# Loading Q and K of the first pairs on two queues, dummy matmuls in TensorE's idle time, and newly searched orders, in a cosine-similarity attention

## The chip, the core and the metric

The kernel runs on one core of one Trainium2 chip. The metric is the device time of one execution in microseconds (us); lower is better. A profile comes from one execution, and its span is about 1.7 us shorter than the time of that same execution (195.7 against 197.39 us for the kernel before, 192.3 against 194.01 for the changed one), so spans are compared only with spans and times only with times.

Runs over 1.5% above the fastest run of the same kernel count as slow and are left out. Two runs are compared as a ratio with a 95% interval, from fast runs of the same rounds.

## The reference, cut to what matters

```python
batch, heads, seq, dim = 8, 12, 512, 64          # Q, K, V: float32, random; tau = 0.1
Q_norm = Q / (np.linalg.norm(Q, axis=-1, keepdims=True) + 1e-10)
K_norm = K / (np.linalg.norm(K, axis=-1, keepdims=True) + 1e-10)
scores = np.einsum('bhqd,bhkd->bhqk', Q_norm, K_norm) / tau
weights = np.exp(scores - np.max(scores, axis=-1, keepdims=True))
weights = weights / (np.sum(weights, axis=-1, keepdims=True) + 1e-10)
return np.einsum('bhqk,bhkd->bhqd', weights, V).astype(np.float32)
```

There are 96 independent heads with 512 rows of 64 each. Each head needs 512 x 512 exponentials, and these are the bulk of the work of ScalarE, which is busy for 94% of the span (its timeline is below).

## The kernel before: the parts that matter

The kernel takes the heads two at a time, as 48 "pairs". Each pair goes through this chain (the short names are those of the printed orders below):

| name | what | engine |
|---|---|---|
| LD.s.0, LD.s.1, LV.s | load Q, K, V of pair s, 256 KB each | a DMA queue |
| SQ | squares of Q and K | GpSimd, in the first pairs also ScalarE |
| SSQ, RED | sums of the squares: 16 matmuls against an identity, then a reduction | TensorE, VectorE |
| LN, EX | 1/norm by logarithm and exponential, pairs 0 and 1 only (later: Newton steps on VectorE) | ScalarE |
| SCL | Q and K scaled to bf16 | VectorE, GpSimd |
| TR, EVA | transposes, and their eviction | TensorE, VectorE |
| SCO.s.c | block c of 4 of the scores: 2 matmuls | TensorE |
| EXP.s.c | exponentials of that block, a 128x1024 tile | ScalarE |
| PV, RCP, NRM, ST | product with V, division by the sums, store | TensorE, VectorE, a DMA queue |

Pair 0 is special. To start early, its K is not scaled ahead of the transposes; the exponential applies 1/norm instead, as a scale for each partition. The partitions of a score tile are 128 rows of K, and the two heads that stand side by side in a tile of 128x1024 ("full tile") need different scales. So the program gives pair 0 eight tiles of 128x512 ("half tiles", 0.69 us each in the trace below) where the others have four full ones.

Every engine executes a fixed, printed list of operations, found earlier by a search. The program adds semaphore waits only where an operation needs another engine's result. So an operation waits for its own operands, and also for **everything ahead of it in its engine's list** (in the trace below the operands of pair 0's first scores are ready at 8.64 us, and these run at 11.48, behind what is listed ahead of them). That second wait is what most of this study is about.

```python
    P.add("table", "act", [], lambda e: e.preload_act_table_set("natural_log_exp_and_others"))
    P.add("wz", "dve", [], lambda e: e.memset(warm_in[:, :], 0.0))
    for k in range(WARM):                                  # WARM = 32
        P.add(("warm", k), "pe", ["wz", ("warm", k - 1) if k else None],
              lambda e: e.matmul(out=sc_ps[:, 3, 0:256], lhsT=warm_in[:, 0:128], rhs=warm_in[:, :], start=True, stop=True))
    ...
        # head of pair 0: K on SyncE's queue
        P.add(("LD", 0, 1), "sp", [], lambda e: e.dma_start(out=qk[0][:, 1], in_=src(K, 0)), slot="first2")
    ...
            # loads of the other pairs: pair 1 on ScalarE's queue, pairs 1 and 2 held back by dummies
            for w, x in ((0, Q), (1, K)):
                P.add(("LD", s, w), "act" if s == 1 else "sp",
                      [key(n, s - R_QK, *y) for n in ("SCL", "SQ") for y in ((w,), (0,), (w, 0), (w, 1))]
                      + [("warm", 2) if s == 1 else ("warm", 9) if s == 2 else None],
                      lambda e, w=w, x=x: e.dma_start(out=qk[iq][:, w], in_=src(x, s)), slot=...)
    ...
ORDER = {
    "sp":  LD.0.1 LD.0.0.1 LD.0.0.0 LD.3.1 LD.2.0 LD.2.1 LD.4.0 ...
    "act": table LD.1.1 LD.1.0 SQ.0.0.1 SQ.0.0.0 SCL.0.1 LN.0.0 EX.0.0 SQ.3.1 SQ.1.0 LN.0.1 EX.0.1 LN.1 EX.1.1 EX.1.0
           EXP.0.0.0 ... EXP.0.2.0 SQ.3.0 EXP.0.2.1 ...
    "pe":  warm.0 ... warm.21 TR.0.1 TR.0 warm.22 ... warm.26 SSQ.1 warm.27 ... warm.30 SCO.0.0 warm.31 SSQ.2 SCO.0.1 TR.1 ...
```

The "warm" matmuls, called dummies below, compute nothing that is used. They are there to keep TensorE busy while it waits for the first data: in the trace below its granted clock falls to 0.50 at 8.56 us, after 3.41 us in which it was busy for 1.66 us.

## Time and profile before

| | us |
|---|---|
| time, median of 3 runs | 196.32 (195.83 to 197.01) |
| span of the profiled run (its time was 197.39) | 195.7 |
| first half tile of pair 0 starts | 12.13 |
| first of the 187 full tiles starts | 18.17 |
| the 187 full tiles, from their start to that of the last three half tiles | 172.8 |
| from there to the end of the span ("tail") | 4.7 |

The last four rows add up to the span (12.13 + 6.04 for pair 0 + 172.79 + 4.74 = 195.7), since ScalarE's exponentials are the one stream that is nearly unbroken from the first score block to the end. Everything else matters only where it delays this stream. Note that the profiled run was about 1.1 us above the median of the timed runs; that matters for the reading of the result.

These are lines of the page of the kernel before: the span, the granted TensorE clock (the share of full rate that the profile records, in tenths) in 40 equal slices, the group of the full tiles (busy us, mean ns | idle just before them, and its cause), the chain of work that ended last, by engine, and two DMA issues with their us to landing.

```profile
span 195.7 us, 7082 instructions
...
PEclk9859999999999999999999999999999999999999
...
ACT 58%; PE 13%; DMA 11%; POOL 7%; DVE 7%; SPq 2%; issue 2%; DVEq 0%; POOLq 0%
...
L451 ACT ACTIVATE et<-scps 128x1024 bf16<-128x1024 f32 x187 | 171.9, 1125 | 1.2 <-PE scps L429 1.2
...
qk<-in_K_dram ACTq DMA_DIRECT2D x1, 256.0 KB, 5.1
qk<-in_Q_dram ACTq DMA_DIRECT2D x1, 256.0 KB, 6.2
```

The full tiles waited only 1.2 us in 173, so a gain has to come from ahead of 18.17 us. The third clock slice (9.8 to 14.7 us) reads 5: TensorE ran at half its rate there. The two loads of pair 1, issued on ScalarE's queue, took 5.1 and 6.2 us to land.

The timeline of ScalarE before (start us, length us, engine, line, operation, out<-in, shapes, count; in brackets the idle time ahead of it and what ended it):

```profile
1.96 0.42 ACTq L377 DMA_DIRECT2D qk<-in_K_dram  x1
2.41 0.49 ACTq L377 DMA_DIRECT2D qk<-in_Q_dram  x1
...
8.46 1.15 ACT L226 ACTIVATE sq<-qk 128x512 bf16<-128x512 f32 x2 [1.47 <-DMA qk<-in_K_dram]
...
12.13 1.26 ACT L441 ACTIVATE et<-scps,xr 128x512 bf16<-128x512 f32 x2 [0.62 <-PE scps L429]
13.85 1.26 ACT L441 ACTIVATE et<-scps,xr 128x512 bf16<-128x512 f32 x2 [0.46 <-PE scps L429]
15.36 0.69 ACT L441 ACTIVATE et<-scps,xr 128x512 bf16<-128x512 f32 x1 [0.24 <-PE scps L429]
15.95 0.62 ACT L226 ACTIVATE sq<-qk 128x512 bf16<-128x512 f32 x1
16.46 1.83 ACT L441 ACTIVATE et<-scps,xr 128x512 bf16<-128x512 f32 x3
18.17 36.75 ACT L451 ACTIVATE et<-scps 128x1024 bf16<-128x1024 f32 x40
...
190.96 1.32 ACT L447 ACTIVATE et<-scps 128x512 bf16<-128x512 f32 x3
```

Pair 1's loads are issued only at 1.96 and 2.41 us. The two squares at 8.46 are pair 3's K and, behind it, pair 1's Q; they end at 9.6. Pair 0's half tiles stall three times (0.46, 0.24, and 0.62 ahead of the first), and a square of pair 3 (0.62 at 15.95) stands among them.

The timeline of TensorE before, same columns:

```profile
9.66 1.03 PE L243 MATMUL xps<-sq,ident 128*128 128x64 bf16 x16 [0.91 <-ACT sq L226]
10.51 1.04 PE L219 MATMUL scps<-warm_in 128*128 128x256 bf16 x4
11.48 0.61 PE L429 MATMUL scps<-qt 64*128 64x512 bf16 x2
```

Pair 0's first scores start at 11.48. They stand in the list behind pair 1's sums (9.66), which waited for ScalarE's square, and behind four dummies. ScalarE had the norms by then and waited 0.62 us for these scores, so that part of the delay is the four dummies'. So the first exponential of pair **0** is set by the loads and squares of pair **1**, and by dummies that stand in front of needed work. Two lines of a table of stretches show the clock (stretch, length, then busy us and instruction count of TensorE, its weight loads, VectorE, ScalarE and GpSimd; then granted clock, DMA share, GB/s):

```profile
5.37:8.78 3.41, 1.64 (x16) 0.86 (x13) 2.37 (x5) 1.61 (x5) 1.43 (x2) 0.97 1.06 367
8.78:12.20 3.42, 2.54 (x23) 1.52 (x24) 0.88 (x2) 1.70 (x8) 2.71 (x3) 0.50 1.09 346
```

TensorE was busy for 1.64 of 3.41 us, and then ran at a clock of 0.50. (The trace's record of the clock has the fall at 8.56 us, just inside the first stretch, and the return to full rate at 15.38. In the 3.41 us up to the fall, from the record's entry at 5.14 us on, TensorE was busy for 1.66 us.)

### The profile page before, as it was taken

What the parts mean: (1) busy time and instruction counts of PE and PEld (TensorE: products, weight loads), DVE (VectorE), ACT (ScalarE), POOL (GpSimd) and SP (SyncE); (2) the same over time, 40 slices, a digit from 0 to 9 for tenths busy, and PEclk for the clock granted to TensorE, in tenths of its full rate; (3) what the DMA queues carried; (4) which work ended last, traced back from release to release, by engine and by line L of the source; (5) the groups of instructions that cost most, each with busy time, mean ns of one, the idle gap of its engine ahead of it and who ended that gap; (6) DMA issues with size and microseconds to landing.
All of it is one profiled execution on the core that took longest, in us unless ns stands there. A gap on an engine that the chain in (4) does not pass through costs nothing.

```text
span 195.7 us, 7082 instructions
## 1 busy us (share of the span) xinstructions
PE 180.5 (92%) x2932; PEld 117.3 (60%) x2932; DVE 149.9 (77%) x450; ACT 183.2 (94%) x212; POOL 161.2 (82%) x148
## 2 busy tenths in 40 slices
PE   7497999999999999999999999999999998999992
PEld 5264676665666666656666665666665665556552
DVE  1448989987888888777888896888797886878534
ACT  3559999999999999999999999999999998999993
POOL 3499899798879999999997999899899969954200
PEclk9859999999999999999999999999999999999999
DMA  4999999999998999999998899569992680555454
GB/s 124 354 348 348 349 344 307 353 195 279 372 381 297 270 297 359 348 344 261 368 383 264 206 358 315 170 173 321 285 318 65 172 282 10 162 153 145 164 170 157
DMA packets 56240, 51.71 MB, mean 264 GB/s; under 512 B 6928, under 2 KB 56208, under 8 KB 56208
## 3 DMA queue, kind: packets, MB, share of 16 engines
q1 hardware_dynamic: 55520, 50.67, 82.9%
q10 hardware_dynamic: 688, 0.59, 1.0%
q8 instruction: 23, 0.38, 0.9%
q14 instruction: 9, 0.07, 0.1%
HBM read 37.75 MB, written 12.58 MB: 257 GB/s over the span
## 4 chain that ended last, share of the span: by engine, by line
ACT 58%; PE 13%; DMA 11%; POOL 7%; DVE 7%; SPq 2%; issue 2%; DVEq 0%; POOLq 0%
ACT et L451 55%; PE scps L429 4%; DMA out_dram<-ob 4%; DMA qt<-qn 4%; PE ops L467 3%; DMA qk<-in_K_dram 3%; POOL qn L267 3%; PE xps L243 3%; POOL sq L228 3%; DVE ob L481 2%; DVE qt L419 1%; ACT et L441 1%; PE xps L274 1%; POOL vb L456 1%; ACT sq L226 1%
## 5 line engine op out<-in xcount | busy, mean ns | idle before, releaser
L451 ACT ACTIVATE et<-scps 128x1024 bf16<-128x1024 f32 x187 | 171.9, 1125 | 1.2 <-PE scps L429 1.2
L228 POOL TENSOR_TENSOR sq<-qk 128x1024 bf16<-128x1024 f32 (+1 forms) x48 | 86.9, 1822 | 8.1 <-DMA qk<-in_K_dram 5.2
L429 PE MATMUL scps<-qt 64*128 64x512 bf16 x384 | 75.5, 390 | 4.8 <-ACT et L451 3.1
L467 PEld LDWEIGHTS ops<-vb,et 128*128 128x128 bf16 x1504 | 53.4, 98 | 27.5 <-issue 21.7
L467 PE MATMUL ops<-vb,et 128*128 128x65 bf16 x1504 | 68.4, 195 | 0.9 <-DVE nps L250 0.5
L267 POOL TENSOR_TENSOR qn<-qk,rk 128x512 bf16<-128x512 f32 x44 | 45.3, 1043 | 9.6 <-DVE rk L343 9.5
L481 DVE TENSOR_TENSOR ob<-ops,rd 128x512 f32<-128x512 f32 x47 | 32.5, 691 | 2.1 <-DMA out_dram<-ob 0.7
L267 DVE TENSOR_TENSOR qn<-qk,nps 128x512 bf16<-128x512 f32 x48 | 32.1, 681 | 0.4
L419 DVE COPY qt<-xps 128x1024 bf16<-128x1024 bf16 (+1 forms) x47 | 30.3, 645 | 2.2 <-PE xps L274 1.6
L456 POOL TENSOR_SCALAR vb<-vf 128x512 bf16<-128x512 f32 x48 | 29.5, 627 | 2.8 <-DMA vf<-in_V_dram 2.8
L429 PEld LDWEIGHTS scps<-qt 64*128 64x128 bf16 x384 | 18.6, 93 | 21.5 <-ACT et L451 7.7
L274 PE MATMUL xps<-ident,qn 128*128 128x128 bf16 x352 | 28.3, 223 | 0.7 <-DVE qn L267 0.7
L243 PE MATMUL xps<-sq,ident 128*128 128x64 bf16 x624 | 25.8, 195 | 3.1 <-ACT sq L226 1.9
L243 PEld LDWEIGHTS xps<-sq,ident 128*128 128x128 bf16 x624 | 21.4, 98 | 11.1 <-issue 4.2
L274 PEld LDWEIGHTS xps<-ident,qn 128*128 128x128 bf16 x352 | 20.2, 99 | 10.1 <-DVE rd L479 3.6
L479 DVE RECIPROCAL rd<-ops 128x8 f32<-128x8 f32 x47 | 9.7, 207 | 17.9 <-PE ops L467 16.9
L250 DVE TENSOR_REDUCE nps<-xps 128x16 f32<-128x64 f32 x38 | 8.8, 231 | 8.1 <-PE xps L243 7.7
L237 DVE TENSOR_REDUCE nps<-sq 128x8 f32<-128x512 bf16 x16 | 10.9, 684 | 0.0
L338 DVE TENSOR_TENSOR nps<-nps,ys 128x32 f32<-128x32 f32 (+1 forms) x48 | 9.3, 194 | 1.1
L339 DVE SCALAR_TENSOR_TENSOR nps<-nps,ys 128x32 f32<-128x32 f32 (+1 forms) x48 | 9.3, 194 | 1.1
L219 PE MATMUL scps<-warm_in 128*128 128x256 bf16 x32 | 6.7, 383 | 1.1 <-DVE warm_in L216 1.1
L226 ACT ACTIVATE sq<-qk 128x512 bf16<-128x512 f32 (+1 forms) x5 | 2.6, 539 | 4.7 <-DMA qk<-in_Q_dram 3.2
(40 smaller groups left out, 43.3 us busy)
## 6 DMA issues: line engine op xcount, KB each, us to landing
vf<-in_V_dram SPq DMA_DIRECT2D x48, 256.0 KB, 6.3
qk<-in_K_dram SPq DMA_DIRECT2D x47, 256.0 KB, 6.2
out_dram<-ob SPq DMA_DIRECT2D x47, 256.0 KB, 4.7
qk<-in_Q_dram SPq DMA_DIRECT2D x46, 256.0 KB, 6.4
qk<-in_Q_dram SPq DMA_DIRECT2D x2, 128.0 KB, 3.2
qk<-in_K_dram ACTq DMA_DIRECT2D x1, 256.0 KB, 5.1
qk<-in_Q_dram ACTq DMA_DIRECT2D x1, 256.0 KB, 6.2
out_dram<-ob SPq DMA_DIRECT2D x1, 128.0 KB, 1.7
```

The lines of the kernel that those rows point to most:

```text
L228: emit = lambda e: e.tensor_tensor(out=b, in0=a, in1=a, op=ALU.mult)
L237: lambda e, w=w: e.tensor_reduce(out=dst(w), in_=sq[s % R_SQ][:, 8 * w : 8 * w + 8, :], axis=AX.X, op=ALU.add))
L243: last = e.matmul(out=x_ps[:, 0:64], lhsT=ident[:, :], rhs=sq[s % R_SQ][:, :, 4 * k : 4 * k + 4], start=(k == 0), stop=(k == 15))
L267: lambda e: e.tensor_tensor(out=qn[iqn][:, w].rearrange("p t h d -> p h t d"), in0=qk[iq][:, w].rearrange("p h (t d) -> p h t d", t=NT), i ...
L274: last = e.transpose(dst[:, i, :], qn[s % R_QN][:, b // NT, b % NT].rearrange("p h d -> p (h d)"), ident[:, :])
L419: lambda e: e.tensor_copy(out=qt[iqt][:, :].rearrange("p w t x -> p (w t) x")[:, 0:nb], in_=tb[:, 0:nb]))
L429: last = e.matmul(out=sc_ps[:, 2 * b + h, :], lhsT=qt[iqt][64 * h : 64 * h + 64, 1, c, :], rhs=qt[iqt][64 * h : 64 * h + 64, 0, :, :], sta ...
L451: lambda e, c=c, b=b: e.activation(out=et[iet][:, c, :, :], in_=sc_ps[:, 2 * b : 2 * b + 2, :], func=ACT.Exp, scale=inv_tau))
L456: lambda e: e.tensor_scalar(out=vb[:, iq, :, :, 0:DIM].rearrange("p c h d -> p h c d"), in0=vf[iv][:, :, :].rearrange("p h (c d) -> p h c ...
L467: last = e.matmul(out=o_ps[:, h, 65 * t : 65 * t + 65], lhsT=et[iet][:, c, h, 128 * t : 128 * t + 128], rhs=vb[:, iq, c, h, :], start=(c = ...
L479: lambda e: e.reciprocal(out=rd[io][:, :], in_=grid[:, :, :, DIM]))
L481: lambda e: e.tensor_tensor(out=ob[io][:, :], in0=grid[:, :, :, 0:DIM], in1=rd[io][:, :].unsqueeze(3).to_broadcast([128, 2, NT, DIM]), op= ...
```

## The change

The intent is threefold: to load Q and K of pairs 0 to 2 at once and in the order of need, K on ScalarE's queue and Q on SyncE's, with no dummy holding a load back; to keep TensorE's clock up by placing the dummies in its predicted idle time up to the first product with V; and to search the printed orders anew, with that load order kept. The core of the diff, with cuts marked by dots:

```
-    for k in range(WARM):
-        P.add(("warm", k), "pe", ["wz", ("warm", k - 1) if k else None],
-              lambda e: e.matmul(out=sc_ps[:, 3, 0:256], lhsT=warm_in[:, 0:128], rhs=warm_in[:, :], start=True, stop=True))
+    def dummy(key, bank, needs):
+        P.add(key, "pe", needs, lambda e: e.matmul(
+            out=bank[:, 0:256], lhsT=warm_in[:, 0:128], rhs=warm_in[:, :], start=True, stop=True))
+    for k in range(WARM):
+        dummy(("warm", k), sc_ps[:, 3], ["wz", ("warm", k - 1) if k else None])
...
-        P.add(("LD", 0, 1), "sp", [], lambda e: e.dma_start(out=qk[0][:, 1], in_=src(K, 0)), slot="first2")
+        P.add(("LD", 0, 1), "act", [], lambda e: e.dma_start(out=qk[0][:, 1], in_=src(K, 0)), slot="first2")
...
-                P.add(("LD", s, w), "act" if s == 1 else "sp",
-                      [key(n, s - R_QK, *y) for n in ("SCL", "SQ") for y in ((w,), (0,), (w, 0), (w, 1))]
-                      + [("warm", 2) if s == 1 else ("warm", 9) if s == 2 else None],
+                P.add(("LD", s, w), "act" if w and s < 3 else "sp",
+                      [key(n, s - R_QK, *y) for n in ("SCL", "SQ") for y in ((w,), (0,), (w, 0), (w, 1))],
...
+    for k in range(sum(FILL)):
+        dummy(("fill", k), *((sc_ps[:, 3], ["wz"]) if k < FILL[0] else (o_ps[:, 0], [("EVA", 0, 1)])))
...
-SQ_ON = {1: ('act', 'pool'), 2: ('act', 'pool'), 3: ('act', 'pool')}
+SQ_ON = {1: ('act', 'pool'), 2: ('act', 'pool')}
-WARM = 32
+WARM = 19
+FILL = (9, 16)
...
 "sp":
-  LD.0.1 LD.0.0.1 LD.0.0.0 LD.3.1 LD.2.0 LD.2.1 LD.4.0 ...
+  LD.0.0.0 LD.0.0.1 LD.1.0 LD.2.0 LV.0 LD.3.1 LD.3.0 ...
 "act":
-  table LD.1.1 LD.1.0 SQ.0.0.1 SQ.0.0.0 SCL.0.1 LN.0.0 EX.0.0 SQ.3.1 SQ.1.0 LN.0.1 EX.0.1 LN.1 EX.1.1 EX.1.0 EXP.0.0.0 ...
+  table LD.0.1 LD.1.1 LD.2.1 SQ.0.0.1 SQ.0.1 LN.0.0 EX.0.0 LN.0.1 SQ.1.1 EX.0.1 SQ.2.1 LN.1 EX.1.0 EX.1.1 EXP.0.0.0 ...
 "pe":
-  warm.0 .. warm.21 TR.0.1 TR.0 warm.22 .. 26 SSQ.1 warm.27 .. 30 SCO.0.0 warm.31 SSQ.2 SCO.0.1 TR.1 SCO.0.2 ...
+  warm.0 .. warm.18 fill.0 TR.0.1 fill.1 .. 4 TR.0 fill.5 .. 8 SSQ.1 SCO.0.0 SCO.0.1 SSQ.2 fill.9 .. 15 TR.1 SCO.0.2
+  fill.16 17 SCO.0.3 fill.18 .. 23 SCO.1.0 SSQ.3 fill.24 PV.0.0.0 ...
 "sp", its end:
-  ST.44 ST.39 ST.45 ST.43 ST.46 ST.47.0 ST.47.1
+  ST.44 ST.39 ST.45 ST.46 ST.42 ST.47.1 ST.47.0
```

Cut here: the waits of a few operations on certain dummies, which now name the last warm-up dummy or are gone; six squares and scales of pairs 0 to 2 that swap ScalarE and GpSimd; and the rest of the printed lists, which the search reordered throughout. Pair 3's squares go to GpSimd as one operation.

> **What bounds the kernel.** ScalarE's exponentials. ScalarE's timeline shows the first half tile at 12.13 us, the eight halves of pair 0 until 18.17, then 187 full tiles until 190.96 (172.8 us, 0.924 each; 0.918 in the chain's longest unbroken stretch, 61.53 us for 67), then 4.7 us of tail. ScalarE's waits put only 1.2 us in front of the full tiles: what can be won lies before 18.17.
>
> **The head before.** Pair 1 decides it. Its loads are held back by dummy matmuls, issued on ScalarE's queue at 1.96 and 2.41 us, and take 5.1 and 6.2 us (DMA issues). DMA moves only 111 to 297 GB/s from 3.5 to 5.5 us (windows). ScalarE's squares (pair 3's K ahead of pair 1's Q) end at 9.6, pair 1's sum matmuls run 9.66 to 10.69, and pair 0's scores stand behind them and four dummies in TensorE's order: 11.48, although their operands were ready at 8.64. The granted clock is 0.5 from about 8.8 to 14 us: 16 sum matmuls take 1.03 us instead of 0.64, eight transposes 1.03 instead of 0.62.
>
> **What changes.** K of pairs 0 to 2 goes on ScalarE's queue, Q on SyncE's, without holds, ahead of other loads. [...] I count on earlier issue and order, not bandwidth. K of pair 0 follows the table load; before's trace has a ScalarE issue at 1.96, ahead of that load's end at 2.06, so I expect it near 1 us. Pair 3's two squares leave ScalarE (0.52 in the stream of pair 0) for GpSimd (1.9 us). 25 fill matmuls follow 19 warm-up ones; they cost time only where TensorE is on the chain: seven stand between pair 2's sums and pair 1's transposes, 0.8 us at full clock, 1.5 at half. [...]
>
> **On the critical path (estimates from those durations).** Pair 1 landed about 7.1; its sums end about 8.5; pair 2's square on ScalarE (landed about 8.5) stands before pair 1's logarithm; first exponential about 9.8 (-2.3). Pair 0 in 5.2 us instead of 6.0 (square gone, a short stall left): first full tile about 15.0 (-3.2). The full tiles lose about 0.5: GpSimd (3.55 us per pair against ScalarE's 3.68) and VectorE have less lead, so pairs 3 to 6 may stall. Tail unchanged.
>
> **Predicted: 193.5 us**, range 191.8 to 195.5. Faster by over 2%: 0.25; within 2%: 0.72; slower by over 2%: 0.03.
>
> **Right or wrong in the profile.** First exponential between 9 and 10.5 us; first full tile 14.3 to 16; K of pair 0 issued near 1 us; granted clock 1.0 from 9 to 14 us, with 0.6 us sums and transposes; 187 full tiles in 172.5 to 174 us; ScalarE's idle in front of them 1 to 2.5 us.
>
> **What would make it wrong.** Landing times: nine loads outstanding within 4 us may delay pairs 1 and 2. K of pair 0 may wait for the table load (+1 us). TensorE may still be throttled. The new order may lack slack in pairs 2 to 6 and give the gain back as stalls. If landings are quick and nothing stalls: 191.5, over 2%.

Two passages are cut from the prediction because no trace or run of this case showed what they rest on. No term of its sum is among them: -2.3, -0.8 and +0.5 us stand, about -2.7 unrounded, which leads from the 196.32 us of before to about 193.5. That the second queue brings no bandwidth was the author's assumption at that point; experiment 3 tests it. The 0.8 and 1.5 us for seven dummies are estimates of the author's: in before's trace the first 22 dummies took 4.53 us, 0.206 each and so 1.4 for seven. In the trace of the changed kernel, at a granted clock of 1.00, the seven took 0.93 us (at 10.10).

## The result, and the profile after

| | before | after |
|---|---|---|
| time, median (range) | 196.21 us (195.83 to 197.01), 4 runs | 193.87 us (193.34 to 194.07), 4 runs |
| span of the profiled run | 195.7 | 192.3 |
| first half tile of pair 0 | 12.13 | 9.59 |
| first full tile | 18.17 | 14.21 |
| 187 full tiles, start to end | 172.79 | 172.44 |
| tail | 4.7 | 5.6 |

The ratio of the times is 0.9871, with a 95% interval of 0.9834 to 0.9908: 1.3% faster, within 2%. A ratio here is the mean time of one kernel's fast runs over the mean of the other's fast runs of the same rounds, so it is not quite the ratio of the medians quoted.

Lines of the page of the kernel after, as above:

```profile
span 192.3 us, 7111 instructions
...
PEclk9999999999999999999999999999999999999998
...
ACT 67%; POOL 15%; PE 8%; DMA 3%; DVE 2%; issue 2%; SPq 0%
...
L453 ACT ACTIVATE et<-scps 128x1024 bf16<-128x1024 f32 x187 | 172.2, 1135 | 0.3
```

The dip of the clock is gone. The chain of work holds less DMA (3% instead of 11%) and more GpSimd (15% instead of 7%).

ScalarE's timeline after:

```profile
0.81 1.28 ACT L215 ACT_TABLE_LOAD   x1 [0.81 <-PEq L694]
0.84 0.46 ACTq L296 DMA_DIRECT2D qk<-in_K_dram  x1
...
6.19 0.61 ACT L229 ACTIVATE sq<-qk 128x512 bf16<-128x512 f32 x1
...
7.38 0.63 ACT L229 ACTIVATE sq<-qk 128x512 bf16<-128x512 f32 x1 [0.49 <-DMA qk<-in_K_dram]
9.12 0.21 ACT L259 ACTIVATE xl<-xs 128x16 f32<-128x16 f32 x1 [1.11 <-DVE xs L253]
...
9.59 4.76 ACT L443 ACTIVATE et<-scps,xr 128x512 bf16<-128x512 f32 x8
14.21 172.56 ACT L453 ACTIVATE et<-scps 128x1024 bf16<-128x1024 f32 x187
186.65 1.18 ACT L449 ACTIVATE et<-scps 128x512 bf16<-128x512 f32 x3
```

The first K is issued at 0.84 us, next to the table load rather than behind it. Pair 1's K is squared at 6.19, pair 2's at 7.38. The eight half tiles and the 187 full tiles each run as one group, with no wait shown between them.

TensorE's timeline and GpSimd's, after:

```profile
8.19 0.65 PE L246 MATMUL xps<-sq,ident 128*128 128x64 bf16 x16 [0.66 <-POOL sq L231]
8.76 0.60 PE L431 MATMUL scps<-qt 64*128 64x512 bf16 x4
```

```profile
7.09 1.04 POOL L231 TENSOR_TENSOR sq<-qk 128x512 bf16<-128x512 f32 x1 [2.38 <-DMA qk<-in_Q_dram]
```

Pair 1's Q lands at 7.09 (before: about 8.6, from its issue at 2.41 plus 6.2). Its square on GpSimd takes 1.04 us, and the sums start at 8.19, 1.47 us earlier than before. At full clock they take 0.65 instead of 1.03 us. The scores follow at once.

So the traces differ by 3.4 us in span: the head up to the first half tile gave 2.54, pair 0 took 4.62 instead of 6.04 us and gave 1.42, the full tiles gave 0.35, and the tail took 0.91 back. The timed difference is 2.5 us (196.3 against 193.8, the means of the four runs each). The rest lies mainly in which execution was profiled: the profiled run of before took 197.39 us, about 1 us over the mean of the timed ones, and the profiled run after (194.01) was close to its own. The full tiles of before's profiled run stalled for 1.2 us, and those of the same lists in experiments 5 and 7 for 0.4; so the 0.35 us of the full tiles is not what a typical run gained there (see the last part).

### The profile page after: what moved, and what is told of

Its sections match the earlier page's. It is cut to its first block, busy times and chain, and to the rows that moved or that the text cites. A ratio compares the mean times of both kernels' runs of the same rounds, so it can differ in the third digit from the quotient of the medians.

```text
span 192.3 us, 7111 instructions
## 1 busy us (share of the span) xinstructions
PE 179.5 (93%) x2944; PEld 117.6 (61%) x2944; DVE 148.3 (77%) x450; ACT 182.3 (95%) x210; POOL 161.8 (84%) x149
## 4 chain that ended last, share of the span: by engine, by line
ACT 67%; POOL 15%; PE 8%; DMA 3%; DVE 2%; issue 2%; SPq 0%
ACT et L453 67%; POOL sq L231 8%; POOL qn L270 4%; DMA qk<-in_Q_dram 3%; POOL vb L458 3%; PE scps L431 2%; PE ops L469 2%; PE xps L246 2%; PE ops L218 1%; PE xps L277 1%; DVE ob L513 1%; PE nps L498 0%; SPq L294 0%; DVE ob L483 0%; POOL vb L212 0%
## 5 line engine op out<-in xcount | busy, mean ns | idle before, releaser
L453 ACT ACTIVATE et<-scps 128x1024 bf16<-128x1024 f32 x187 | 172.2, 1135 | 0.3
L231 POOL TENSOR_TENSOR sq<-qk 128x1024 bf16<-128x1024 f32 (+2 forms) x48 | 87.5, 1837 | 4.2 <-DMA qk<-in_Q_dram 4.2
L431 PE MATMUL scps<-qt 64*128 64x512 bf16 x384 | 74.7, 386 | 4.4 <-ACT et L453 2.4
L246 PE MATMUL xps<-sq,ident 128*128 128x64 bf16 x624 | 24.9, 192 | 2.0 <-POOL sq L231 0.9
L246 PEld LDWEIGHTS xps<-sq,ident 128*128 128x128 bf16 x624 | 20.8, 97 | 8.9 <-issue 3.8
L481 DVE RECIPROCAL rd<-ops 128x8 f32<-128x8 f32 x47 | 9.7, 206 | 15.6 <-PE ops L469 15.2
L218 PE MATMUL scps<-warm_in 128*128 128x256 bf16 x28 | 5.8, 384 | 1.1 <-DVE warm_in L216 1.1
L218 PEld LDWEIGHTS scps<-warm_in 128*128 128x128 bf16 x28 | 3.7, 138 | 2.3 <-DVE warm_in L216 1.1
```

The source lines that it names most:

```text
L218: P.add(key, "pe", needs, lambda e: e.matmul(out=bank[:, 0:256], lhsT=warm_in[:, 0:128], rhs=warm_in[:, :], start=True, stop=True))
L231: emit = lambda e: e.tensor_tensor(out=b, in0=a, in1=a, op=ALU.mult)
L246: last = e.matmul(out=x_ps[:, 0:64], lhsT=ident[:, :], rhs=sq[s % R_SQ][:, :, 4 * k : 4 * k + 4], start=(k == 0), stop=(k == 15))
L431: last = e.matmul(out=sc_ps[:, 2 * b + h, :], lhsT=qt[iqt][64 * h : 64 * h + 64, 1, c, :], rhs=qt[iqt][64 * h : 64 * h + 64, 0, :, :], sta ...
L453: lambda e, c=c, b=b: e.activation(out=et[iet][:, c, :, :], in_=sc_ps[:, 2 * b : 2 * b + 2, :], func=ACT.Exp, scale=inv_tau))
```

## The experiments

The theory going in: three things together make the gain, namely loads that land earlier, in the order of need; a TensorE at full clock from 9 to 14 us; and orders that keep ScalarE's stream unbroken once it starts earlier. The rivals: only one of these matters (the loads, or the dummies); the second queue itself gives bandwidth; the later reordering alone does it. There were twelve runs, in three calls (1 to 4, then 5, 7 and two of 9, then 6, 8 and the last of 9; the first call was on another chip than the other two); all gave correct outputs. The kernel before ran in each call, with fast-run means of 196.17, 195.82 and 196.16 us. In the first call 4 of its 11 runs were slow (197.54 to 198.27), in the second 2 of 11; they are left out.

For comparison, the ten timed runs of the changed kernel (four above, six in the experiment on its repetition) lie between 193.34 and 194.45 us. Single traces scatter too: in four traces with its head (its own two, and two with only the stores moved) the first half tile starts at 9.59, 9.25, 9.26 and 9.10 us, and the first full tile at 14.21, 13.88, 13.88 and 13.73.

### 1. The last stores in another order (a_stores)

```
 changed kernel, "sp", its end:
-  ST.44 ST.39 ST.45 ST.46 ST.42 ST.47.1 ST.47.0
+  ST.44 ST.39 ST.42 ST.45 ST.46 ST.47.0 ST.47.1
```

> The changed kernel with two stores reordered: pair 42's store goes out before pair 45's instead of after pair 46's, and the two pieces of the last pair's first head go out in the order in which they are finished. Theory 1 (the tail of the changed kernel, 5.65 us from the last full tile to the end against 4.74 before, is long because pair 42's 256 KB stand in front of the last stores): the tail falls to 4.6 to 5.0 us and the time by 0.6 to 1.0 us (193.9 to about 193.1). Rival (the last stores are slow for another reason, such as the landing of the last 64 KB on ScalarE's queue): the tail stays at 5.4 us or more and the time within 0.2 us. The head is untouched: first exponential 9.6 us, first full tile 14.2 us.

Measured: 193.36 us median, ratio to before 0.987 (0.9816 to 0.9924). The tail was 5.18 us in its trace, against 5.65 in the trace of the changed kernel; that is in neither of the two ranges expected. The time can't be told from the changed kernel's across calls, so this was repeated later side by side (experiment 8).

### 2. No dummies in the idle time (b_nofill)

```
-FILL = (9, 16)
+FILL = (0, 0)
 and every fill.k out of TensorE's list
```

> The changed kernel without its 25 fill matmuls (the 19 warm-up ones stay). Theory 1 (the fills keep TensorE's clock, and the clock is worth something in the head): the granted clock shows 0.5 for one or two stretches between 6 and 16 us, 16 sums take about 1.0 us and eight transposes 1.0 us there, the first full tile starts 0.4 to 1.2 us later than 14.2, and the time rises by 0.4 to 1.2 us. Rival (landing times, VectorE and GpSimd set the head; TensorE has slack either way): the first full tile within 0.2 us of 14.2 and the time within 0.3 us, whatever the clock does.

Measured: 194.88 us mean of the five fast runs (194.06 to 195.79; one slow run, 197.59, left out), ratio 0.9944 (0.9883 to 1.0004). That is about 1 us worse than the changed kernel (0.9 to 1.1, by the means of its two sets of runs), and the ranges barely overlap. The changed kernel did not run in this call; the one-queue version of experiment 3, which equals it in time, did, and lies 1.2 us lower. ScalarE's and TensorE's timelines show where:

```profile
13.20 2.42 ACT L443 ACTIVATE et<-scps,xr 128x512 bf16<-128x512 f32 x4 [0.72 <-PE scps L431]
15.49 172.37 ACT L453 ACTIVATE et<-scps 128x1024 bf16<-128x1024 f32 x187
```

```profile
8.29 1.04 PE L246 MATMUL xps<-sq,ident 128*128 128x64 bf16 x16 [0.97 <-POOL sq L231]
...
14.94 0.65 PE L246 MATMUL xps<-sq,ident 128*128 128x64 bf16 x16
```

The same 16 sum matmuls take 1.04 us at 8.29 and 0.65 us at 14.94, so TensorE still ran at half rate at 8.29, and at full rate by 14.94. Half tile 5, the first of the group at 13.20, waits 0.72 us for its scores, and the first full tile starts at 15.49 instead of 14.21. The dummies in the idle time are a needed part of this kernel; the rival that they do nothing falls. But it is left with 19 dummies, where the kernel before had 32, so this measures having the 25, not their new places. And experiment 6 reached full rate without a fill.

A trap lies here: the profile gives this trace a granted clock of 1.00 in every stretch of 1 us from 2 to 16 us, although the durations say half rate at 8.29. The kernel before has something similar: the record of the clock in its trace begins at 5.14 us, and the stretches from 1 to 5 us are given 1.00, yet the first 22 dummies took 0.206 us each, where in the changed kernel seven took 0.93 us (0.13 each) at 10.10. Durations of a known instruction are the safer reading.

### 3. All loads on one queue (c_onequeue)

```
 changed kernel:
-        P.add(("LD", 0, 1), "act", ...)            +        P.add(("LD", 0, 1), "sp", ...)
-   P.add(("LD", s, w), "act" if w and s < 3 else "sp", ...   +   P.add(("LD", s, w), "sp", ...
-"sp":  LD.0.0.0 LD.0.0.1 LD.1.0 LD.2.0 LV.0 ...
+"sp":  LD.0.0.0 LD.0.0.1 LD.0.1 LD.1.0 LD.1.1 LD.2.0 LD.2.1 LV.0 ...
-"act": table LD.0.1 LD.1.1 LD.2.1 SQ.0.0.1 ...
+"act": table SQ.0.0.1 ...
```

> The changed kernel with K of pairs 0 to 2 issued on SyncE's queue too, in the order Q, K of pair 0, 1, 2; ScalarE issues no load. Theory 1 (two queues are worth only the issue time; from 2.5 us on the transfers are limited by what the engines move, 330 to 380 GB/s): K of pair 0 is issued at about 1.7 instead of 0.84 us and lands 0.5 us later, but Q of pair 1, on which the changed kernel's chain hangs, is issued at about 2.2 instead of 1.7 us and lands within 0.5 us of 7.0, since K of pair 2 no longer shares the engines with it; first exponential 9.3 to 10.1 us, time within 0.5 us. Rival (the second queue is what makes the head short): first exponential at 10.6 us or later and time up by 1 us or more.

Measured: 193.64 us mean (192.94 to 194.56), ratio 0.988 (0.9828 to 0.9933): nothing lost that these runs can resolve. The first half tile started at 9.57 and the first full tile at 14.20, against 9.59 and 14.21. K of pair 0 landed later (4.73, against 4.08), and so did K of pair 2 (8.59, against 7.38), but Q of pair 1 landed earlier (GpSimd squared it at 5.48 without a wait, against 7.09), and it cancels out. The 330 to 380 GB/s of the expectation are near what the trace of the changed kernel has from 3 to 7 us (328 to 381 GB/s in each half us); that this limits the transfers was the author's estimate. So the second queue itself is not what helps. What is left of this part of the change is the **order** of the loads and the missing holds.

### 4. The holds put back (d_holds)

```
-                      [key(n, s - R_QK, *y) for n in ("SCL", "SQ") for y in (...)],
+                      [key(n, s - R_QK, *y) for n in ("SCL", "SQ") for y in (...)]
+                      + [("warm", 2) if s == 1 else ("warm", 9) if s == 2 else None],
```

> The changed kernel with the holds of the kernel before put back: pair 1's loads wait for the third dummy matmul (about 1.9 us), pair 2's for the tenth (about 3.4 us). Theory 1 (issuing without holds is the main gain of the head): pair 1 lands 0.3 to 0.8 us later and pair 2 1.2 us later, DMA shows a dip after 3.5 us; first exponential 10.0 to 10.8 us, first full tile 14.8 to 16 us, time up by 0.5 to 1.5 us. Rival (the order and the split of the loads make the gain, the holds only keep the first pair clear): pair 0 lands earlier, first exponential within 0.3 us of 9.6, time within 0.3 us.

Measured: 194.88 us mean (194.35 to 196.46, all fast), ratio 0.9944 (0.9884 to 1.0003), about 1 us worse than the changed kernel. One run (196.46, at a granted clock of 0.983, the others at 0.995 or more) makes part of that: the other five average 194.57, some 0.6 to 0.9 us worse. The reason differs from the one I had: pair 1 did not land later (GpSimd squared its Q at 6.74, earlier than 7.09). ScalarE's timeline shows what did:

```profile
9.29 0.63 ACT L229 ACTIVATE sq<-qk 128x512 bf16<-128x512 f32 x1 [1.70 <-DMA qk<-in_K_dram]
9.82 0.20 ACT L259 ACTIVATE xl<-xs 128x16 f32<-128x16 f32 x1
...
10.27 4.75 ACT L444 ACTIVATE et<-scps,xr 128x512 bf16<-128x512 f32 x8
```

K of pair **2**, held back further, lands at 9.29 instead of 7.38. Its square stands in ScalarE's list ahead of pair 1's logarithm, whose sums had ended at 8.48, and which ran only at 9.82, right behind the square. All eight half tiles then start 0.68 us later than in the first trace of the changed kernel (1.2 us later than in the earliest of the four).

### 5. The loads alone, on the kernel before (e_before_loads)

```
 kernel before: K of pairs 0 to 2 to "act", Q to "sp", no holds
-"sp":  LD.0.1 LD.0.0.1 LD.0.0.0 LD.3.1 LD.2.0 LD.2.1 LD.4.0 ...
+"sp":  LD.0.0.1 LD.0.0.0 LD.1.0 LD.2.0 LD.3.1 LD.4.0 ...
-"act": table LD.1.1 LD.1.0 SQ.0.0.1 ...
+"act": table LD.0.1 LD.1.1 LD.2.1 SQ.0.0.1 ...
```

> One part of the change alone: the kernel before with only its first loads changed (K of pairs 0 to 2 on ScalarE's queue, Q on SyncE's, pair 1 before pair 3, no holds); no fill, and every other order as before. Theory 1 (the loads are worth 0.5 to 1 us by themselves, as putting the holds back into the changed kernel cost 0.7 us at the first full tile): pair 1's square on ScalarE ends at 8.8 to 9.3 us instead of 9.6, still behind the square of pair 3's K, the first full tile starts 0.3 to 1.0 us before 18.2, and the time falls by 0.3 to 1.0 us. Rival (the loads alone are worth the whole gain): first full tile before 16 us, time down by 2 us or more.

Measured: 197.05 us mean, ratio 1.0063 (1.0027 to 1.0098): **slower** than before. ScalarE's timeline:

```profile
8.88 1.15 ACT L226 ACTIVATE sq<-qk 128x512 bf16<-128x512 f32 x2 [3.27 <-DMA qk<-in_K_dram]
```

Pair 1 had landed long before; GpSimd had squared its K at 5.88. But in the old list pair 3's K is squared ahead of pair 1's Q, and pair 3's load is now behind more others. ScalarE waited 3.27 us for it. The clock fell to half again (sums of 1.03 us at 10.09; granted clock 0.56 from 8.78 to 12.2 us and 0.50 from there to 15.6). Five of its six runs have a granted clock of 0.978 to 0.983, lower than most of before's, so how much of the loss is the clock's was not separated. The gain that was expected here did not come.

### 6. The loads, and the squares in the order of landing (l_loads_squares)

```
 e_before_loads, "act":
-  EX.0.0 SQ.3.1 SQ.1.0 LN.0.1 EX.0.1 LN.1 EX.1.1 EX.1.0 EXP.0.0.0 EXP.0.0.1 ...
+  EX.0.0 SQ.1.0 LN.0.1 EX.0.1 LN.1 EX.1.1 EX.1.0 EXP.0.0.0 SQ.3.1 EXP.0.0.1 ...
```

> e_before_loads with one more thing: on ScalarE, pair 3's K is squared after pair 0's first exponential instead of ahead of pair 1's square. e_before_loads waited there 3.3 us for pair 3's K although pair 1 had landed. Theory 1 (early loads are worth something only where the order of use follows the order of arrival): pair 1's square starts by 7.2 us, first exponential 9.6 to 10.6 us, first full tile 15.5 to 16.6, time down by 1 to 2.5 us against e_before_loads (197.0), with a spread of 1 us or more, as the clock is not looked after. Rival (without the fills nothing is won): first full tile at 17.5 us or later.

Measured: 195.01 us mean, ratio 0.9937 (0.9893 to 0.9981), from the third call. ScalarE's timeline, and one line of VectorE's:

```profile
15.07 17.51 ACT L451 ACTIVATE et<-scps 128x1024 bf16<-128x1024 f32 x19
33.10 19.52 ACT L451 ACTIVATE et<-scps 128x1024 bf16<-128x1024 f32 x21 [0.52 <-PE scps L429]
53.57 36.80 ACT L451 ACTIVATE et<-scps 128x1024 bf16<-128x1024 f32 x40 [0.96 <-PE scps L429]
90.69 98.22 ACT L451 ACTIVATE et<-scps 128x1024 bf16<-128x1024 f32 x107 [0.31 <-PE scps L429]
```

```profile
51.62 0.69 DVE L481 TENSOR_TENSOR ob<-ops,rd 128x512 f32<-128x512 f32 x1 [1.29 <-DMA out_dram<-ob]
```

One moved square on top of the moved loads, and the head is 3.1 us shorter than before (15.07 against 18.17). The first half tile starts at 8.99 us, earlier than in any trace of the changed kernel, and the sums even ran at full clock (0.64 us at 7.55) without a fill; they followed five dummies after 0.06 us, but why the clock was up was not shown. But the full tiles now stall for 1.8 us: 0.52 + 0.96 + 0.31. The largest stall comes when VectorE's division waits 1.29 us for an output buffer whose store had not finished; stores stand among the loads in SyncE's list, and that list was made for a later start (that this is why the store was late is argued, not tested). Beside the changed kernel in the same call (experiment 8) this trace is 1.0 us longer: its first half tile is 0.26 us earlier, but pair 0 takes 1.45 us more (both squares of pair 3 stand in it, and a stall of 0.34), the full tiles take 0.70 us more, and the tail 0.9 less. So a third part is needed: orders, those inside pair 0 and the later ones, that fit the earlier start. The full tiles of the changed kernel idle for 0.3 us in its trace, and for 0.8 in the trace of its repetition.

This does not mean that the old lists are worse as such. With the old, late start the same later lists stalled only 0.36 us (experiment 5) and 0.38 us (the next one), though 1.2 us in before's own trace.

### 7. Sixteen dummies alone, on the kernel before (f_before_fill)

```
 kernel before, "pe":
-  warm.21 TR.0.1 TR.0 warm.22 ... warm.26 SSQ.1
+  warm.21 fill.0 .. 3 TR.0.1 fill.4 .. 7 TR.0 warm.22 ... warm.26 fill.8 .. 15 SSQ.1
```

> The other part alone: the kernel before with 16 more dummy matmuls (4 before and 4 between pair 0's two transposes, 8 in front of pair 1's sums), everything else as before. Theory 1 (dummies keep TensorE at full rate, and the spread of the kernel before, 194.4 to 198.3 us in 11 runs against 192.9 to 194.6 in 19 of the variants with fills, comes from the clock): sums of 0.64 us and transposes of 0.62 us from 8 us on, first full tile 0.8 to 1.8 us earlier than 18.2, median down by 1 us or more from the 197.2 of the last job, and the runs within 1 us of each other. Rival (the spread is of the chip or of the loads): the spread stays at 2 us or more, the median within 0.5 us.

Measured: 195.06 us mean (194.64 to 195.78), ratio 0.9966 (0.9927 to 1.0004): about 0.8 us better, though the interval just includes no change. In its trace the sums took 0.65 and the transposes 0.61 us, the eight half tiles ran without a stall, the first started at 11.14 (before: 12.13) and the first full tile at 16.41 (before: 18.17). The same stretch of 5.37 to 8.78 us had TensorE busy 3.11 of 3.41 us, against 1.64 before. Two lines of ScalarE's timeline:

```profile
16.41 36.76 ACT L451 ACTIVATE et<-scps 128x1024 bf16<-128x1024 f32 x40
...
188.19 1.32 ACT L447 ACTIVATE et<-scps 128x512 bf16<-128x512 f32 x3
```

The trace of before is from a run above its median, so 1.8 us is the upper end of what the dummies gave on a typical run. How often before's clock falls can be read from the mean granted clock on record for each run. Of before's 27 fast runs in the three calls, 4 have 0.980 to 0.983 (196.5 to 197.5 us), 17 have 0.986 to 0.991 (194.5 to 197.3 us) and 6 have 0.996 or more (194.4 to 197.2 us); the six runs with the dummies have 0.996 to 1.000. A mean of 0.991 is, as an estimate, 3.5 us at half rate (the stretch at 0.50 at the end of a trace accounts for 1.9 us in that of the changed kernel, from 190.40 us on, and for an estimated 2.3 us at most in the other traces with a mean of 0.994 or more), so before's clock fell in most of its runs. The spread, too, was smaller, as expected: 1.1 us here, 2.1 us for the nine fast runs of before in the same call. That the clock makes the spread is not shown by this, since before's runs at 0.996 or more are not faster than those at 0.991.

### 8. The change and the stores' order, side by side (j_after_again, k_stores_again)

The first is the changed kernel, unedited; the second is experiment 1 again, in the same call.

> The changed kernel unaltered, on the chip of this job, to be compared with the store version beside it: 193.3 to 194.1 us, spread under 1 us, first full tile 13.9 to 14.3, last full tile to the end 5.4 to 5.8 us.

> The same kernel as a_stores, beside the changed kernel on one chip. If pair 42's late store costs what the first trace said, 0.4 to 0.8 us below j_after_again; if that was the landing of one run, within 0.2 us of it.

Measured: the changed kernel 193.99 us mean, ratio 0.9884 (0.9845 to 0.9924); with the stores moved 193.42 us, ratio 0.9858 (0.9814 to 0.9903). The difference is 0.57 us, inside the 0.4 to 0.8 expected, with overlapping ranges (193.66 to 194.45, and 192.99 to 194.10). The two traces differ by more, 0.9 us in span, of which the tail is 0.4, the full tiles 0.3 and the head 0.15. The last group of exponentials on ScalarE's timeline, of the changed kernel again and then of the moved stores:

```profile
186.74 1.18 ACT L449 ACTIVATE et<-scps 128x512 bf16<-128x512 f32 x3
```

```profile
186.25 1.18 ACT L449 ACTIVATE et<-scps 128x512 bf16<-128x512 f32 x3
```

The spans were 192.3 and 191.4, so the tails were 5.6 and 5.2 us. Over all traces: 5.56 to 5.65 with pair 42's store in the last place (4.9 on one queue is the exception, not explained), 5.0 to 5.2 with it moved. What the 0.57 us of the timed runs consists of is not shown beyond that.

### 9. Pair 0 ahead of pair 1's sums (g_front, h_front_pool, i_front2)

These three try to start the exponentials still earlier, all with the stores moved.

```
 g_front, on k_stores_again:
 "pool": -SCL.0.1 SQ.1.0 vone SQ.2.0 SCL.1.1 VC.0 SQ.3.0      +SCL.0.1 vone SQ.1.0 SQ.2.0 VC.0 SCL.1.1 SQ.3.0
 "dve":  -EVA.0 EVA.0.1 RED.1.0                               +EVA.0.1 EVA.0 RED.1.0
 "pe":   -SSQ.1 SCO.0.0 SCO.0.1                               +SCO.0.0 SSQ.1 SCO.0.1
 "act":  -EX.0.1 SQ.2.1 LN.1 EX.1.0 EX.1.1 EXP.0.0.0 EXP.0.0.1 EXP.0.1.0
         +EX.0.1 EXP.0.0.0 SQ.2.1 EXP.0.0.1 LN.1 EX.1.0 EX.1.1 EXP.0.1.0
 h_front_pool: the same, and SCL.5.1 (scale of pair 5's K) from "pool" to "dve"
 i_front2: g_front, and in "pe"
         -SSQ.2 fill.9 .. 15 TR.1 SCO.0.2 fill.16 17 SCO.0.3        +SSQ.2 SCO.0.2 fill.9 .. 15 SCO.0.3 TR.1 fill.16 17
         -SSQ.9 SCO.4.3                                             +SCO.4.3 SSQ.9
```

> A version meant to beat both: the changed kernel with the stores of a_stores, and a new order at the front: pair 0's first scores before pair 1's sums on TensorE, two of pair 0's exponentials before pair 1's logarithm on ScalarE, GpSimd's constant fill in its wait for pair 1, the value cast in its wait for pair 1's norms. Theory 1 (ScalarE's start alone sets the time): first exponential at 7.7 to 8.3 us, first full tile 13.1 to 13.6, no stall over 0.3 us after it, time 192.3 to 192.8. Rival (GpSimd is as tight as ScalarE up to about 50 us, as the chain of waits of the changed kernel has it): first exponential as early, but ScalarE stalls 0.5 us or more in front of the full tiles before 60 us, and the time falls by 0.4 us or less against a_stores (193.4).

> g_front with pair 5's K scaled on VectorE (0.68 us) instead of GpSimd (1.04 us). If GpSimd is the second limit (the rival of g_front), the stalls before 60 us shrink by 0.3 to 1.0 us against g_front and the time by as much; if ScalarE's start alone sets the time, there is no difference, or a loss of up to 0.5 us from a busier VectorE.

> g_front with three TensorE positions changed: pair 0's third and fourth score blocks go ahead of pair 1's transposes, and pair 4's last score block ahead of pair 9's sums. g_front lost 1.09 us in front of pair 0's fifth half because the third block stood behind seven fills and the transposes. Theory 1 (that order was all that cost g_front its gain): no stall inside pair 0 over 0.3 us, first full tile 13.4 to 13.9, later stalls under 0.4 us together, time 192.4 to 193.0, below the store version. Rival (GpSimd and VectorE, which start pair 3 no earlier than in the changed kernel, are as tight as ScalarE): the first full tile is early, but the stalls before 60 us grow by as much as was won, and the time is within 0.3 us of the store version.

Measured: g_front 194.22 us mean (ratio 0.9918, 0.9886 to 0.9951), h_front_pool 194.72 (0.9943, 0.9911 to 0.9976), i_front2 193.50 (0.986, 0.9821 to 0.9899). None beats the plain version with the stores moved (193.42 and ratio 0.9858; i_front2 ran in the same call, the other two in another one), though their exponentials start at 7.95 to 8.15 us, against 9.59 in the trace of the changed kernel and 9.10 with the stores moved. ScalarE's timeline of g_front:

```profile
7.95 0.69 ACT L443 ACTIVATE et<-scps,xr 128x512 bf16<-128x512 f32 x1 [1.14 <-PE scps L431]
...
12.41 2.42 ACT L443 ACTIVATE et<-scps,xr 128x512 bf16<-128x512 f32 x4 [1.09 <-PE scps L431]
14.71 172.60 ACT L453 ACTIVATE et<-scps 128x1024 bf16<-128x1024 f32 x187
```

The start moved from 9.10 (the trace with the stores moved) to 7.95, and the gain was lost at once: half tile 5 needs the third score block, which stands behind pair 2's sums, seven dummies and pair 1's transposes (0.50 us of waiting for GpSimd's scale), and starts at 11.98. The first full tile came later (14.71, against 13.73). i_front2 moved that score block up; its ScalarE timeline:

```profile
13.58 2.15 ACT L453 ACTIVATE et<-scps 128x1024 bf16<-128x1024 f32 x2
15.94 2.85 ACT L453 ACTIVATE et<-scps 128x1024 bf16<-128x1024 f32 x3 [0.21 <-PE scps L431]
19.02 41.78 ACT L453 ACTIVATE et<-scps 128x1024 bf16<-128x1024 f32 x45 [0.23 <-PE scps L431]
60.99 125.86 ACT L453 ACTIVATE et<-scps 128x1024 bf16<-128x1024 f32 x137 [0.18 <-PE scps L431]
```

The first full tile is at 13.58, and the full tiles stall 0.62 us in place of 0.22 with the stores alone. What was won ahead (0.15 us at the first full tile) was given back behind. In h_front_pool, VectorE became the late one: transposes waited 0.45 us for its scale of pair 5. This fits the view that, with an earlier start, neither GpSimd nor VectorE has room in the first pairs; it does not show it.

## Why the prediction was right

The predicted time, 193.5 us, is 0.4 us from the median of 193.87, inside the range given, and the change was within 2%, as thought most likely. By terms of the sum:

| term | predicted | traced |
|---|---|---|
| up to the first half tile | -2.3 | -2.54 |
| pair 0 | -0.8 (6.0 to 5.2 us, a short stall left) | -1.42 (4.62 us, no stall) |
| full tiles | +0.5 | -0.35 (against other traces of the old lists +0.7, below) |
| tail | 0 | +0.91 |
| sum | about -2.7 | -3.40 in span, about -2.5 in time |

**Right in mechanism and size: the head.** K of pair 0 was issued at 0.84 (predicted near 1). Pair 1 landed at 7.09 (about 7.1). Its sums ended at 8.84 (about 8.5) and took 0.65 us at full clock. The clock read 1.00 from 9 to 14 us, and this time the durations agree with it. The first half tile started at 9.59 (about 9.8). One queue instead of two lost nothing, as "I count on earlier issue and order, not bandwidth" has it: 193.64 us with one queue, 193.79 and 193.99 with two.

**Right, with another link.** "Pair 2's square on ScalarE (landed about 8.5) stands before pair 1's logarithm" was not what set the first exponential: pair 2's K landed at 7.38, and pair 1's logarithm waited for its sums (1.11 us, by the line at 9.12). The link is real, as the holds showed (experiment 4): there K of pair 2 landed at 9.29 and delayed everything by 0.68 us.

**Ranges missed by a little.** The first full tile came at 14.21 us (14.3 to 16 foreseen), and the 187 full tiles took 172.44 us (172.5 to 174).

**Mis-sized.** "A short stall left" in pair 0: none was. The TensorE work between pair 0's score blocks, 0.93 us for seven dummies among it, stayed hidden behind exponentials of 0.6 us per half tile. Experiment 7 splits the 1.42 us: with before's lists at full clock pair 0 took 5.27 us, without a stall and with pair 3's square still in it. So 0.77 us came with the clock and 0.65 with what is left, the square above all (0.52 predicted).

**Against one trace wrong, against the others right: the full tiles.** "The full tiles lose about 0.5": against the profiled run of before, their stretch was 0.35 us shorter. But that was a run with 1.2 us of stalls, 0.64 of them ahead of the tile at 165.43 us. The same lists took 171.76 and 171.78 us in experiments 5 and 7 (in 7 from 16.41 to 188.19), and the seven traces with the changed kernel's later lists, with starts of 13.73 to 15.49, took 172.24 to 172.86. So the full tiles did lose, 0.5 to 1.1 us. The way was not the predicted one: stalls of 1 to 2.5 us were foreseen, and the idle was 0.3 us (0.8 in the repetition); ScalarE was busy for 172.2 us in the tiles against 171.7 in experiments 5 and 7, and why is not known. With the orders of before and the early start the loss was 1.8 us (experiment 6, 173.56 us).

**Wrong: "Tail unchanged".** It took 0.9 us more. Kernels with the new orders had a tail of about 5.6 us, with one exception; taking pair 42's store out of the place just ahead of pair 47's brought it to 5.0 to 5.2; kernels with the old orders have 4.7. The remaining 0.3 to 0.5 us was not traced further.

**What was luck.** The head and pair 0 gave 0.86 us more than predicted, and the tail, which the prediction left out, took 0.91 us; that the two cancel brought the number so near. As an estimate for a typical run of before, with 171.78 us for its full tiles, the terms are -2.54 - 1.42 + 0.66 + 0.91 = -2.4 us, close to the timed 2.5.

What the gain consists of, then, on the runs: the missing holds (0.6 to 1 us), the dummies in idle time (about 1 us), and orders to match, without which the loads alone made it slower (+0.6%). These are not independent terms to be summed: the first two were each measured with the rest of the change present.

**Still open.** Which of the many reorderings keeps which tile from stalling was not separated. Two parts of the change had no run of their own: that pair 0's scores no longer stand behind four dummies (0.62 us of waiting before), and that six squares and scales changed engines. The landing of the same load varied by 0.3 to 0.5 us between runs of kernels with the same head, without a cause found. The spread looks smaller with the dummies: ten runs of the changed kernel and six of experiment 7 each lie within 1.1 us, the 27 fast runs of before within 3.1 us (194.41 to 197.49). But experiment 5's runs, without the new dummies, lie within 1.3 us, and experiment 4's, with them, within 2.1, so the cause is not shown.

The version with the stores moved (k_stores_again), at 193.42 us or 1.4% below before, is the fastest of those measured, though its lead over the changed kernel lies within overlapping ranges.

## What to carry to other kernels

In a kernel whose engines run fixed lists, an operation waits for what stands ahead of it, so ask of each early operation what is ahead of it in its list and when *that* one's data lands; loads moved without the list that consumes them made this kernel slower. A head that is shortened must be followed by orders that fit the earlier start, or part of the gain can come back as stalls, some of them tens of microseconds later (1.8 us in experiment 6). Read TensorE's clock from the length of a known matmul group, since the recorded clock can show full speed where the durations do not (experiment 2: 1.00 while the 16 sums took 1.04 us, against 0.65 later).

## What the traces show besides

- TensorE's clock. In the trace of the kernel before, the record of the clock has entries at 5.14 us (1.00), 8.56 (0.50) and 15.38 (1.00), that is 3.41 and 6.83 us apart. TensorE was busy for 1.66 us of the 3.41 up to the fall, with no gap over 1.1 us; for 2.51 of the next 3.41, after which the clock stayed at 0.50; and for all of the 3.41 after that, at whose end full rate came back. In the trace of the changed kernel it was busy for 2.47 of 3.41 us (6.08 to 9.49) and the clock stayed at 1.00. In experiment 5 it was busy for 1.75 of 3.41 us (5.37 to 8.78), and the stretch after that had a granted clock of 0.56. These are single traces; at what busy share the clock turns is not shown. The busy times are the profile's, whose matmul ends are modelled.
- A DMA issue on ScalarE's queue inside a table load. In the trace of the changed kernel the load of the table took 1.28 us (0.81 to 2.09), and the first issue on ScalarE's queue came at 0.84 us, inside it.
- From issue to use or landing. In the trace of the changed kernel the first load of 128 KB, on SyncE's queue, was in use 2.44 us after its issue (0.80 to 3.24). The median from issue to landing was 2.7 us for the two loads of 128 KB, 4.7 us for the three of 256 KB on ScalarE's queue, and 6.0 us for the 47 of Q of 256 KB, most of them issued later.
